# Two-layer encoder: the seam between the first MLP and mixer B with scratch moved, TensorE's order written out and weight splits queued later

## The chip, the core and the metric

The kernel runs on one core of a Trainium2 chip. Its time is the device time of one execution in microseconds; of several executions the median is taken. The profile is of one execution.

## The reference

The input is x (1, 512, 1024) in float32. Two layers follow each other; each is a token mixer and a squared-ReLU MLP, both with a norm ahead and added to the residual. Layer 0 has mixer A (dilated sliding-window attention), layer 1 has mixer B (latent attention), which is where the change lies:

```python
def mla_mixer(h, w_in, q_a_gain, w_qb, kv_a_gain, w_kvb, q_gain, k_gain, w_o):
    lat = h @ w_in                                   # (512, 448)
    c_q, c_kv, k_rope = lat[..., :256], lat[..., 256:384], lat[..., 384:]
    q = (rms_norm(c_q, q_a_gain) @ w_qb).reshape(B, S, 8, 192)
    kv = (rms_norm(c_kv, kv_a_gain) @ w_kvb).reshape(B, S, 8, 256)
    k_nope, v = kv[..., :128], kv[..., 128:]
    k = concatenate([k_nope, broadcast(k_rope)], -1)
    q, k = rms_norm(q, q_gain), rms_norm(k, k_gain)
    ... # rope on the last 64 of q and k
    ... # softmax(q k / sqrt(192)) v over all 512 positions, then @ w_o

def reference(x, ...):
    for i in range(2):
        x = x + mixer_i(rms_norm(x, norm_mix[i]), ...)
        x = x + sq_relu_mlp(rms_norm(x, norm_ffn[i]), ffn_w1[i], ffn_w2[i])
    return x
```

## The kernel before

Matrices are multiplied in three passes: each operand is split into a high part, which ScalarE copies, and a low part, which VectorE subtracts, and TensorE adds up high times high, high times low and low times high. `load_unit` (lines 151 to 160) loads a piece of a weight matrix into a `raw` buffer (three of them) and splits it into a `whi` and a `wlo` buffer (four each). The 512 positions are four row tiles of 128.

The seam is the stretch from the end of MLP 0 to the first attention scores of mixer B. These steps follow each other in it:

- The last two Winograd products of MLP 0 add their results to `resid`. When a row tile is complete, `done0` calls `norm_tile`, which makes the normed row `xn` (in one of the two `S` buffers of pool `mlp0`) and returns `turn`: eight transposes on TensorE in two halves, and the split of their result into `hT`. `done0` calls the turn at once.
- `run_block` on line 1166 multiplies `hT` by `b_w_in`: per row tile four steps of six matmuls, 448 columns wide, 24 matmuls in all, into one of the four `acc` accumulators. `evac_lat` then takes a row: three squares with sums on ScalarE, a root by a power on GpSimd (`rstd_of`, line 133), the normed latents `cn` on VectorE with the gains `gl`, three transposes, and the split into `cT`.
- `new_pair(p)` loads and splits the two weight pieces of heads 2p and 2p+1. `kv_chunk` projects one row of keys and values (three matmuls of 512 columns), takes two squares, the power, `ks`, `kd`; its second part transposes them (four transposes) and splits them into `kn` and `kr`. `q_chunk` does the same for one row of queries (six matmuls of 384 columns).
- The loop over `s_` runs 32 scores (five matmuls each) with maximum, exponential, scaling, four transposes three steps later, and the product with the values after each fourth. While a pair's scores run, the chunks of the next pair are made.

Each engine has one queue, filled in an order that a planner works out when the kernel is built: of what it takes to be ready, the first traced goes first. `tc.issue_after(ins)` ties what is traced in its block, on the engine of `ins`, behind `ins` in that queue; a tie is an order and no wait for a result. In `block_groups` the dictionary `between` gives a function that is traced behind the step with that number, tied behind the step's last matmul; if it returns an instruction, the next step is tied behind it.

Memory: pools are a stack. `h1p` holds `hT_f0`, the normed input of MLP 0 (32 KiB per partition), and `mlp0` lies above it with `a2` (16 KiB), four `asp` (32 KiB) and two `S` (8 KiB). When both are closed, `bpool` (17.5 KiB) and `bw` (71.5 KiB) take their place from the bottom, so `bw` as a whole reaches from the last part of `hT_f0` over `a2`, `asp` and `S`. `gl` uses the one buffer of tag `gain`, which until then holds the gains of the mixer's norm.

Of the kernel before, what the change touches and what calls it, by code (L numbers as in the profile page):

```python
# [10 lines left out]
F32 = mybir.dt.float32  # L11
# [77 lines left out]
def encoder_kernel(ctx: ExitStack, tc: tile.TileContext, x, norm_mix, norm_ffn, a_w_qkv, a_q_gain, a_k_gain,  # L89
# [7 lines left out]
    def nm(s):  # L97
        uid[0] += 1
        return f"{s}_{uid[0]}"
# [24 lines left out]
    def transpose(o, i):  # L124
        return PE.transpose(o, i, ident)  # L125
# [832 lines left out]
    with tc.tile_pool(name="mlp0", bufs=1, reuse_waits="tile") as mp:  # L958
        state = {}

        def done0(r, c):
            state[r] = state.get(r, 0) + 1
            if state[r] < 2:
                return
            if r == 0:
                state["g"] = gain_table(norm_mix[1:2, :].rearrange("o d -> (o d)"), D, "g_mix1")
                state["hT"] = new_hT()
            norm_tile(r, resid[:, r], state["g"], state["hT"], mp, xn_tag="S")()
        mlp(0, ffn_w1[0], ffn_w2[0], hT, resid, mp, done0)
# [4 lines left out]
    if True:  # L974
        with tc.tile_pool(name="bpool", bufs=1, reuse_waits="tile") as bp, \
                tc.tile_pool(name="bw", bufs=2, reuse_waits="tile") as bw:
            cosB = ck[:, C_COSB:C_SINB].rearrange("p (r d) -> p r d", r=NT)
            sinB = ck[:, C_SINB:C_COSA].rearrange("p (r d) -> p r d", r=NT)
            gl = gp.tile([P, D], F32, tag="gain", name="gl")
# [20 lines left out]
            def evac_lat(r, acc):  # L1000
                junk = bw.tile([P, QL], F32, tag="junkb", name=nm("junkb"), bufs=1)
                ss = st.tile([P, 8], F32, tag="lss", name=nm("lss"))
                mean_square(junk, acc[:, 0:QL], QL, ss[:, 0:1])
                mean_square(junk[:, 0:KVL], acc[:, QL:QL + KVL], KVL, ss[:, 1:2])
                mean_square(junk[:, 0:RD], acc[:, 384:448], QKD, ssr[:, r:r + 1])
                V.tensor_scalar(ssr[:, r:r + 1], ssr[:, r:r + 1], EPS, None, op0=ALU.add)
                rs = rstd_of(ss[:, 0:2], 2, EPS, "lrs")
                cn = bw.tile([P, QL + KVL], F32, tag="cn", name=nm("cn"))
                V.scalar_tensor_tensor(cn[:, 0:QL], acc[:, 0:QL], rs[:, 0:1], gl[:, 0:QL], op0=ALU.mult, op1=ALU.mult)
                V.scalar_tensor_tensor(cn[:, QL:384], acc[:, QL:384], rs[:, 1:2], gl[:, QL:384], op0=ALU.mult,  # L1010
                                       op1=ALU.mult)
                t2 = bw.tile([P, 2 * RD], F32, tag="kr2", name=nm("kr2"), bufs=1)[:, 0:RD]
                V.tensor_tensor(krr[:, r], acc[:, 384:448], cgB[:, r, 1], op=ALU.mult)
                V.tensor_tensor(t2[:, 0:32], acc[:, 416:448], sgB[:, r, 1, 32:64], op=ALU.mult)
                V.tensor_tensor(t2[:, 32:64], acc[:, 384:416], sgB[:, r, 1, 0:32], op=ALU.mult)
                G.tensor_tensor(krr[:, r], krr[:, r], t2, op=ALU.add)
                tp = tp_p.tile([P, 512], F32, tag="tp", name=nm("tp"))
                for j in range(3):
                    transpose(tp[:, j * P:(j + 1) * P], cn[:, j * P:(j + 1) * P])
                tv = tp[:, :384].rearrange("p (k t) -> p k t", k=3)  # L1020
                hi, lo = cT[:, :, 0, r * P:(r + 1) * P], cT[:, :, 1, r * P:(r + 1) * P]
                A.activation(hi, tv, AF.Copy)
                V.tensor_tensor(lo, tv, hi.bitcast(F32), op=ALU.subtract)
# [6 lines left out]
            def new_pair(p):  # L1030
# [7 lines left out]
                d["wkv"] = load_unit(wkv[:, :, 512 * p:512 * p + 512], 1, None, 512, home=homes[1])  # L1038
                d["wq"] = load_unit(wq[:, :, 384 * p:384 * p + 384], 2, None, 384, home=homes[0])
# [19 lines left out]
            def q_chunk(d, r):  # L1059
# [3 lines left out]
                junk = bw.tile([P, QL], F32, tag="junkb", name=nm("junkb"), bufs=1)  # L1063
# [5 lines left out]
                qs = bw.tile([P, 2, DH], F32, tag="qs", name=nm("qs"), bufs=2)  # L1069
# [29 lines left out]
            def kv_chunk(d, r):  # L1099
                acc = proj(d, "wkv", r, 2, 512)  # L1100
                a4 = acc.rearrange("p (h c d) -> p h c d", h=2, c=2)
                junk = bw.tile([P, QL], F32, tag="junkb", name=nm("junkb"), bufs=1)
# [5 lines left out]
                ks = bw.tile([P, 2, DH], F32, tag="ks", name=nm("ks"), bufs=2)  # L1108
# [20 lines left out]
            def score(d, h, r):  # L1129
# [11 lines left out]
                pe = bw.tile([P, S], F32, tag="pe", name=nm("pe"), bufs=3)  # L1141
                A.activation(pe, sc, AF.Exp, bias=mx[:, 1:2], scale=rq, accum_out=mx[:, 2:3])
# [23 lines left out]
            run_block(w_units(b_w_in[0], 0, 448), [4], 448, act_stationary(hT, 448), evac_lat)  # L1166
            oB = new_hT()
            cur = new_pair(0)
            late = []
            for r in range(NT):  # L1170
                late.append(kv_chunk(cur, r))
                if r == 2:
                    late.append(q_chunk(cur, 0))
                if r:
                    late.pop(0)()
# [74 lines left out]
```

## Time and profile before

| | us |
|---|---|
| median of 3 runs | 1406.21 |
| lowest and highest | 1405.14 and 1407.54 |
| profiled execution, its own time | 1405.79 |
| its span, first to last instruction | 1404.0 |

Times in the views are counted from the first instruction. TensorE (PE), VectorE (DVE), ScalarE (ACT), GpSimd (POOL) and SyncE (SP) work at the same time; an engine's idle time matters only where the chain that ends last runs through it. The time of a matmul in a view holds its way through the array, so that neighbours overlap; what one costs in a row of many is read from the chain.

### The profile page before, as it was taken

To read this page: it belongs to the slowest core of one execution; us is meant where nothing else is said; L and a number is where in the kernel's file an instruction comes from. 1 tells how busy PE (TensorE), PEld (TensorE's weight loads), DVE (VectorE), ACT (ScalarE), POOL (GpSimd) and SP (SyncE) were. 2 spreads that over 40 slices of the span, in tenths; PEclk is the share of its full clock that TensorE was granted. 3 is DMA by queue.
4 is the path that set the end of the run, shared out by engine and by line. 5 is a ranking of instruction groups with operands and counts; after the bars stand their busy time and mean duration, and the time that the engine had idled before them with its cause. 6 is when DMAs were issued, how large, how long until landed. Compare 5 with 4: busy or idle time off the path is not lost.

```text
span 1404.0 us, 18978 instructions
## 1 busy us (share of the span) xinstructions
PE 1371.9 (98%) x6852; PEld 1164.1 (83%) x6852; DVE 940.9 (67%) x1498; ACT 801.2 (57%) x1643; POOL 225.3 (16%) x240
## 2 busy tenths in 40 slices
PE   7999999999999999999999999999999999999998
PEld 6999878888889989888888878777769888888886
DVE  6885777788788744574655769788745465574747
ACT  6543778687786625454536455777534553644543
POOL 1110212121122001020200204433201020020101
PEclk9999999999999999999999999999999999999999
DMA  9535554655555539486583944201116668493835
GB/s 301 172 133 162 131 135 98 164 124 133 143 125 123 159 106 260 142 187 176 121 238 86 235 96 94 61 31 31 46 46 191 170 132 228 100 226 124 200 85 120
DMA packets 171775, 197.83 MB, mean 141 GB/s; under 512 B 59105, under 2 KB 109025, under 8 KB 171681
## 3 DMA queue, kind: packets, MB, share of 16 engines
q1 hardware_dynamic: 152496, 157.55, 37.9%
q0 software_dynamic: 19184, 39.07, 15.5%
q8 instruction: 54, 0.88, 0.3%
q14 instruction: 41, 0.33, 0.1%
HBM read 176.13 MB, written 7.86 MB: 131 GB/s over the span
## 4 chain that ended last, share of the span: by engine, by line
PE 81%; DVE 7%; ACT 4%; DMA 4%; issue 2%; SPq 0%; POOL 0%; ACTq 0%; DVEq 0%
PE acc L188 46%; PE sc L868 11%; PE tp L868 7%; PE tp L125 3%; DMA xT<-t 2%; PE sc L430 2%; PE acc L1161 1%; PE sc L1055 1%; DVE wlo L811 1%; PE acc L1137 1%; PE tp L430 1%; PE sco L710 1%; PE acc L430 1%; PE sco L706 1%; ACT junk L138 1%
## 5 line engine op out<-in xcount | busy, mean ns | idle before, releaser
L188 PE MATMUL acc<-whi,hT 128*128 128x512 f32 (+2 forms) x1208 | 377.2, 388 | 1.9 <-ACT hT L752 1.0
L188 PE MATMUL acc<-hT_f,whi 128*128 128x512 f32 (+1 forms) x1152 | 317.4, 366 | 0.0
L159 DVE TENSOR_TENSOR wlo<-raw,whi 128x1024 fp32r<-128x1024 f32 (+3 forms) x146 | 172.9, 1188 | 164.3 <-ACT whi L158 163.7
L188 PEld LDWEIGHTS acc<-whi,hT 128*128 128x128 f32 x1208 | 224.3, 188 | 43.0 <-ACT hT L1163 1.5
L158 ACT ACTIVATE whi<-raw 128x1024 fp32r<-128x1024 f32 (+3 forms) x146 | 149.6, 1029 | 161.8 <-PE acc L188 72.1
L188 PEld LDWEIGHTS acc<-hT_f,whi 128*128 128x128 f32 x1152 | 207.8, 189 | 34.9
L188 PE MATMUL acc<-wlo,hT 128*128 128x512 f32 (+2 forms) x604 | 233.0, 387 | 0.7 <-DVE wlo L159 0.7
L811 DVE TENSOR_TENSOR wlo<-wqs,whi 128x1024 fp32r<-128x1024 f32 x112 | 137.7, 1231 | 112.9 <-ACT whi L810 112.9
L810 ACT ACTIVATE whi<-wqs 128x1024 fp32r<-128x1024 f32 x112 | 118.3, 1059 | 161.6 <-PE acc L188 65.0
L188 PE MATMUL acc<-hT_f,wlo 128*128 128x512 f32 (+1 forms) x576 | 204.1, 366 | 0.0
L868 PE MATMUL sc<-whi,asp 128*128 128x512 f32 x512 | 165.2, 390 | 1.3 <-DVE resid L842 1.3
L796 POOL DMA_DIRECT2D wqs<-in_ffn_w_dram x64 | 77.6, 1347 | 540.1 <-DVE wlo L811 358.3
L188 PEld LDWEIGHTS acc<-wlo,hT 128*128 128x128 f32 x604 | 113.6, 188 | 20.2 <-DVE wlo L159 1.1
L188 PEld LDWEIGHTS acc<-hT_f,wlo 128*128 128x128 f32 x576 | 108.3, 189 | 17.4
L868 PEld LDWEIGHTS sc<-whi,asp 128*128 128x128 f32 x512 | 96.2, 188 | 21.9 <-issue 2.1
L868 PE MATMUL tp<-whi,asp 128*128 128x512 f32 x352 | 112.2, 390 | 0.9 <-DVE resid L842 0.9
L133 POOL TENSOR_TENSOR qrs<-rs_v,nhalf 128x4 f32<-128x4 f32 x48 | 65.9, 1376 | 264.1 <-DVE rs_v L130 233.2
L868 PE MATMUL sc<-wlo,asp 128*128 128x512 f32 x256 | 99.7, 390 | 0.0
L304 ACT ACTIVATE qkT<-xT 128x1024 uint16<-128x1024 uint16 x48 | 56.4, 1182 | 42.1 <-DMA xT<-t 42.0
L868 PEld LDWEIGHTS tp<-whi,asp 128*128 128x128 f32 x352 | 66.1, 188 | 15.0 <-DVE resid L842 1.3
L868 PE MATMUL tp<-wlo,asp 128*128 128x512 f32 x176 | 68.2, 390 | 0.0
L138 ACT ACTIVATE junk<-acc 128x128 f32<-128x128 f32 x192 | 52.1, 272 | 10.7 <-PE acc L188 7.0
(236 smaller groups left out, 2187.2 us busy)
## 6 DMA issues: line engine op xcount, KB each, us to landing
wqs<-in_ffn_w_dram SPq DMA_DIRECT2D x80, 512.0 KB, 5.2
raw<-in_ffn_w_dram SPq DMA_DIRECT2D x64, 512.0 KB, 4.2
wqs<-in_ffn_w_dram POOLq DMA_DIRECT2D x64, 512.0 KB, 7.5
raw<-in_a_w_qkv_dram SPq DMA_DIRECT2D x96, 256.0 KB, 3.2
b<-in_a_w_qkv_dram SPq DMA_DIRECT2D x24, 384.0 KB, 5.7
vall<-vo POOLq DMA_DIRECT2D x24, 192.0 KB, 2.3
raw<-in_a_w_o_dram SPq DMA_DIRECT2D x8, 512.0 KB, 3.8
raw<-in_b_w_o_dram SPq DMA_DIRECT2D x8, 512.0 KB, 3.8
```

What stands on the lines that cost most here:

```text
L125: return PE.transpose(o, i, ident)
L133: G.tensor_tensor(out, v[:, :n], nhalf[:, :n], op=ALU.pow)
L138: A.activation(junk, x, AF.Square, scale=1.0 / math.sqrt(dim), accum_out=out)
L158: A.activation(hi[:, :nk, :n], raw[:, :nk, :n], AF.Copy)
L159: V.tensor_tensor(lo[:, :nk, :n], raw[:, :nk, :n], hi[:, :nk, :n].bitcast(F32), op=ALU.subtract)
L188: last = PE.matmul(accs[o][:, oc], lhsT=lt, rhs=rt, start=(kt == 0 and p_i == 0 and hv == 0), stop=(kt == total - 1 and p_i == 2), skip_gr ...
L304: A.activation(dst, xT.rearrange("p (h c) t -> p c t h", h=2), AF.Copy)
L430: PE.matmul(banks[t][:, :VH], lhsT=lt, rhs=rt[:, j], start=(first and k == 0 and i_ == 0), stop=(k == 3 and i_ == 2), skip_group_check=True)
L796: marks["sum"] = nc.gpsimd.dma_start(t, src, accum_op=ALU.add).ins
L810: A.activation(hi, x, AF.Copy)
L811: V.tensor_tensor(lo, x, hi.bitcast(F32), op=ALU.subtract)
L868: PE.matmul(bk[t], lhsT=lt, rhs=rt[:, j], start=(first and k == 0 and i_ == 0), stop=(k == 3 and i_ == 2), skip_group_check=True)
```

## The change

Four things are changed. A new pool `bl` is opened between `bpool` and `bw`; it holds `gl`, the scratch of the latents (`junkb`, `kr2`), `qs`, `ks`, and one tag `pe` of three buffers that the latents' `cn` share with the exponentials. It takes 13.5 KiB, so it ends 1 KiB below the end of what `hT_f0` was, and `bw` begins behind it. `done0` keeps the turns of rows 2 and 3 instead of calling them. `evac_lat` ends ahead of its transposes and returns them as a function; the block of the latents gets a `between` that names when each turn, each latent row's transposes and the first keys are issued by TensorE. And `new_pair` loads both of its pieces first and, for every pair but the first, ties ScalarE's half of the splits behind the first exponential of the pair that is running.

```diff
-            norm_tile(r, resid[:, r], state["g"], state["hT"], mp, xn_tag="S")()
+            turn = norm_tile(r, resid[:, r], state["g"], state["hT"], mp, xn_tag="S")
+            if r < 2:
+                turn()
+            else:
+                state[f"turn{r}"] = turn
...
+                tc.tile_pool(name="bl", bufs=2, reuse_waits="tile") as bl, \
...
-            gl = gp.tile([P, D], F32, tag="gain", name="gl")
+            gl = bl.tile([P, 512], F32, name="gl", bufs=1)
...
-                cn = bw.tile([P, QL + KVL], F32, tag="cn", name=nm("cn"))
+                cn = bl.tile([P, S], F32, tag="pe", name=nm("cn"), bufs=3)
...
-                tp = tp_p.tile([P, 512], F32, tag="tp", name=nm("tp"))
-                for j in range(3):
-                    transpose(tp[:, j * P:(j + 1) * P], cn[:, j * P:(j + 1) * P])
...
+                def turn():
+                    tp = tp_p.tile([P, 512], F32, tag="tp", name=nm("tp"))
+                    for j in range(3):
+                        t = transpose(tp[:, j * P:(j + 1) * P], cn[:, j * P:(j + 1) * P])
...
+                    return t.ins
+                return turn
...
-                d["wkv"] = load_unit(wkv[:, :, 512 * p:512 * p + 512], 1, None, 512, home=homes[1])
-                d["wq"] = load_unit(wq[:, :, 384 * p:384 * p + 384], 2, None, 384, home=homes[0])
+                srcs = ("wkv", wkv[:, :, 512 * p:512 * p + 512], 1, 512), ("wq", wq[:, :, 384 * p:384 * p + 384], 2, 384)
+                raws = [load_raw(src, nk, None, n) for _, src, nk, n in srcs]
+                with ExitStack() as behind:
+                    if p:
+                        behind.enter_context(tc.issue_after(marks["exp", 0, 0]))
+                    for i, (name, src, nk, n) in enumerate(srcs):
+                        d[name] = load_unit(src, nk, None, n, home=homes[1 - i], raw=raws[i])
...
-                A.activation(pe, sc, AF.Exp, bias=mx[:, 1:2], scale=rq, accum_out=mx[:, 2:3])
+                marks["exp", h, r] = A.activation(pe, sc, AF.Exp, bias=mx[:, 1:2], scale=rq, accum_out=mx[:, 2:3]).ins
...
-            run_block(w_units(b_w_in[0], 0, 448), [4], 448, act_stationary(hT, 448), evac_lat)
+            lat, late = {}, []
+
+            def first_pair():
+                t = state["turn2"]()
+                state["cur"] = new_pair(0)
+                return t
+
+            def keys(r):
+                late.append(kv_chunk(state["cur"], r))
+
+            run_block(w_units(b_w_in[0], 0, 448), [4], 448, act_stationary(hT, 448),
+                      lambda r, acc: lat.update({r: evac_lat(r, acc)}),
+                      between={4: first_pair, 7: lambda: lat[0](), 8: state["turn3"], 10: lambda: keys(0),
+                               11: lambda: lat[1](), 13: lambda: late.pop(0)(), 14: lambda: keys(1),
+                               15: lambda: lat[2]()})
             oB = new_hT()
-            cur = new_pair(0)
-            late = []
-            for r in range(NT):
-                late.append(kv_chunk(cur, r))
-                if r == 2:
-                    late.append(q_chunk(cur, 0))
-                if r:
-                    late.pop(0)()
+            cur = state["cur"]
+            late.append(q_chunk(cur, 0))
+            keys(2)
+            late.pop(0)()
+            lat[3]()
+            keys(3)
             for f in late:
                 f()
```

`junkb`, `kr2`, `qs`, `ks` and `pe` go from `bw` to `bl` in the same way. The steps of the block count 0 to 15: step 4r + u is unit u of row r.

## Rows read from the trace of the kernel before

**Rows 1.** The page: busy time of each engine, and the chain that ended last, by engine

```profile
PE 1371.9 (98%) x6852; PEld 1164.1 (83%) x6852; DVE 940.9 (67%) x1498; ACT 801.2 (57%) x1643; POOL 225.3 (16%) x240
...
PE 81%; DVE 7%; ACT 4%; DMA 4%; issue 2%; SPq 0%; POOL 0%; ACTq 0%; DVEq 0%
```

**Rows 2.** Windows around the seam: from:to, length, busy of each engine, clock, DMA

```profile
870.00:882.00 12.00, 12.00 (x68) 11.00 (x68) 6.32 (x10) 4.28 (x10) 0.55 (x1) 1.00 0.41 124
...
888.00:904.00 16.00, 13.10 (x73) 10.44 (x72) 13.69 (x48) 13.84 (x60) 10.90 (x18) 1.00 0.40 128
...
904.00:920.00 16.00, 14.60 (x78) 11.32 (x77) 14.16 (x45) 12.30 (x46) 6.43 (x11) 1.00 0.02 7
...
920.00:950.00 30.00, 30.00 (x154) 22.88 (x154) 26.13 (x76) 22.50 (x74) 8.98 (x14) 1.00 0.11 33
...
950.00:1000.00 50.00, 46.91 (x235) 35.01 (x234) 42.92 (x121) 36.88 (x124) 17.29 (x25) 1.00 0.11 32
```

**Rows 3.** TensorE in order of time, 838 to 930: start, length, what, [idle before]

```profile
871.69 0.37 PE L188 MATMUL acc<-whi,hT 128*128 128x448 f32 x1
...
887.90 0.45 PE L188 MATMUL acc<-whi,hT 128*128 128x448 f32 x1
...
894.46 0.33 PE L125 MATMUL tp<-ck,ks 128*128 128x128 f32 x1 [0.59 <-DVE ks L1109]
...
900.04 1.29 PE L1055 MATMUL sc<-w,cT 128*128 128x384 f32 x6 [0.89 <-DVE r L1076]
...
902.92 0.47 PE L1055 MATMUL sc<-whi,cT 128*128 128x512 f32 x1 [0.65 <-DVE rs_v L130]
...
903.69 0.86 PE L1137 MATMUL acc<-kn,qn 128*128 128x512 f32 x3
```

**Rows 4.** ScalarE in order of time, 850 to 925

```profile
880.96 0.60 ACT L234 ACTIVATE hT<-tp 128x512 fp32r<-128x512 f32 x1 [2.08 <-PE tp L125]
...
881.45 0.38 ACT L138 ACTIVATE junkb<-acc 128x256 f32<-128x256 f32 x1
...
889.84 0.85 ACT L158 ACTIVATE whi<-raw 128x768 fp32r<-128x768 f32 x1 [0.42 <-DVE cT L1023]
...
908.69 0.77 ACT L1142 ACTIVATE pe<-acc,bmx,rqs 128x512 f32<-128x512 f32 x1
```

**Rows 5.** The DMA issues of SyncE's queue in order of time, 830 to 925

```profile
874.73 0.55 SPq L980 DMA_DIRECT2D gl<-in_b_q_a_gain_dram  x1
```

**Rows 6.** The chain in order of time, 860 to 881: start, length, instructions

```profile
863.12 2.74 PE sc L868 x12
...
872.06 0.44 PE tp L125 x4
```

**Rows 7.** VectorE in order of time, 850 to 925

```profile
883.68 0.48 DVE L1009 SCALAR_TENSOR_TENSOR cn<-acc,lrs,gl 128x256 f32<-128x256 f32 x1
...
884.08 0.34 DVE L1010 SCALAR_TENSOR_TENSOR cn<-acc,lrs,gl 128x128 f32<-128x128 f32 x1
...
885.83 2.36 DVE L159 TENSOR_TENSOR wlo<-raw,whi 128x512 fp32r<-128x512 f32 x3
...
890.72 0.96 DVE L159 TENSOR_TENSOR wlo<-raw,whi 128x768 fp32r<-128x768 f32 x1 [0.47 <-ACT whi L158]
```

**Rows 8.** Tile cT: what wrote it; min, median, max ns; first and last start

```profile
L1022 ACT ACTIVATE cT<-tp x4: 482/488/493, 888.2 to 894.3; 128x384 fp32r<-128x384 f32 x4
...
L1023 DVE TENSOR_TENSOR cT<-tp,cT x4: 545/546/556, 889.2 to 894.8; 128x384 fp32r<-128x384 f32 x4
```

**Rows 9.** Groups by line and shape, 880 to 932: busy us, mean ns, idle before

```profile
L1111 POOL TENSOR_TENSOR kd<-krr,krs 128x256 f32<-128x256 f32 x8 | 4.9, 615 | 0.4
...
L1122 ACT ACTIVATE kn<-tp,gn 128x256 fp32r<-128x256 f32 x8 | 3.9, 489 | 0.0
```

**Rows 10.** Line L133, the power on GpSimd: min, median, max ns

```profile
L133 POOL TENSOR_TENSOR nrs<-rs_v,nhalf x16: 548/552/1644, 6.0 to 1073.4; 128x1 f32<-128x1 f32 x16
...
L133 POOL TENSOR_TENSOR krs<-rs_v,nhalf x16: 695/698/862, 892.7 to 986.5; 128x2 f32<-128x2 f32 x16
```

More of the change, by code (lines that the diff above doesn't have):

```diff
@@ L1000, in evac_lat @@
             def evac_lat(r, acc):
-                junk = bw.tile([P, QL], F32, tag="junkb", name=nm("junkb"), bufs=1)
+                junk = bl.tile([P, QL], F32, tag="junkb", name=nm("junkb"), bufs=1)
                 ss = st.tile([P, 8], F32, tag="lss", name=nm("lss"))
@@ L1011, in evac_lat @@
                                        op1=ALU.mult)
-                t2 = bw.tile([P, 2 * RD], F32, tag="kr2", name=nm("kr2"), bufs=1)[:, 0:RD]
+                t2 = bl.tile([P, 2 * RD], F32, tag="kr2", name=nm("kr2"), bufs=1)[:, 0:RD]
                 V.tensor_tensor(krr[:, r], acc[:, 384:448], cgB[:, r, 1], op=ALU.mult)
@@ L1016, in evac_lat @@
                 G.tensor_tensor(krr[:, r], krr[:, r], t2, op=ALU.add)
-                tp = tp_p.tile([P, 512], F32, tag="tp", name=nm("tp"))
-                for j in range(3):
-                    transpose(tp[:, j * P:(j + 1) * P], cn[:, j * P:(j + 1) * P])
[L1020 to L1023, printed above, removed]
+                def turn():
+                    tp = tp_p.tile([P, 512], F32, tag="tp", name=nm("tp"))
+                    for j in range(3):
+                        t = transpose(tp[:, j * P:(j + 1) * P], cn[:, j * P:(j + 1) * P])
+                    tv = tp[:, :384].rearrange("p (k t) -> p k t", k=3)
+                    hi, lo = cT[:, :, 0, r * P:(r + 1) * P], cT[:, :, 1, r * P:(r + 1) * P]
+                    A.activation(hi, tv, AF.Copy)
+                    V.tensor_tensor(lo, tv, hi.bitcast(F32), op=ALU.subtract)
+                    return t.ins
+                return turn
             wq = b_w_qb[0].rearrange("(k p) c -> p k c", p=P)
@@ L1062, in q_chunk @@
                 a3 = acc[:, :384].rearrange("p (h d) -> p h d", h=2)
-                junk = bw.tile([P, QL], F32, tag="junkb", name=nm("junkb"), bufs=1)
+                junk = bl.tile([P, QL], F32, tag="junkb", name=nm("junkb"), bufs=1)
                 ss = st.tile([P, 8], F32, tag="qss", name=nm("qss"))
@@ L1068, in q_chunk @@
                 rstd_of(ss[:, 0:2], 2, QKD * EPS, None, d["rq"][:, r])
-                qs = bw.tile([P, 2, DH], F32, tag="qs", name=nm("qs"), bufs=2)
+                qs = bl.tile([P, 2, DH], F32, tag="qs", name=nm("qs"), bufs=2)
                 A.activation(qs, a3[:, :, 0:DH], AF.Copy)
@@ L1101, in kv_chunk @@
                 a4 = acc.rearrange("p (h c d) -> p h c d", h=2, c=2)
-                junk = bw.tile([P, QL], F32, tag="junkb", name=nm("junkb"), bufs=1)
+                junk = bl.tile([P, QL], F32, tag="junkb", name=nm("junkb"), bufs=1)
                 ss = st.tile([P, 8], F32, tag="kss", name=nm("kss"))
@@ L1107, in kv_chunk @@
                 A.activation(d["v"][:, r], a4[:, :, 1], AF.Copy)
-                ks = bw.tile([P, 2, DH], F32, tag="ks", name=nm("ks"), bufs=2)
+                ks = bl.tile([P, 2, DH], F32, tag="ks", name=nm("ks"), bufs=2)
                 V.tensor_tensor(ks, a4[:, :, 0], rs.unsqueeze(2).broadcast_to([P, 2, DH]), op=ALU.mult)
@@ L1140, in score @@
                 V.tensor_scalar(mx[:, 1:2], mx[:, 0:1], rq, -1.0, op0=ALU.mult, op1=ALU.mult)
-                pe = bw.tile([P, S], F32, tag="pe", name=nm("pe"), bufs=3)
-                A.activation(pe, sc, AF.Exp, bias=mx[:, 1:2], scale=rq, accum_out=mx[:, 2:3])
+                pe = bl.tile([P, S], F32, tag="pe", name=nm("pe"), bufs=3)
+                marks["exp", h, r] = A.activation(pe, sc, AF.Exp, bias=mx[:, 1:2], scale=rq, accum_out=mx[:, 2:3]).ins
                 V.reciprocal(mx[:, 3:4], mx[:, 2:3])
```

## The prediction

> **What bounds the kernel now.** The page comes first: TensorE is busy for 98% of the span, and 81% of the chain that ends last is TensorE's own work [rows 1]. A change that leaves TensorE's instructions as they are, as this one does, can only win time in which TensorE stands. The second view is therefore the table of windows: where does TensorE stand, and what do the others do there? From 870 to 882 it is busy for all of 12.00 us, while VectorE works 6.32 and ScalarE 4.28. From 888 to 904 it works 13.10 of 16, and now VectorE (13.69) and ScalarE (13.84) are the full ones; from 904 to 920 it works 14.60 of 16 [rows 2]. So the seam loses 2.9 + 1.4 = 4.3 us, and just ahead of the loss two engines are half idle. The clock is 1.00 in all these windows; it plays no part.
>
> The third view is the order of time. The last matmul of latent row 0 starts at 871.69, so row 0 is complete at 871.9 [rows 3]. Its first square starts on ScalarE only at 881.45, right behind the copy of the last normed row's transposes, for which ScalarE had stood 2.08 us [rows 4]. Row 0 waits 9.6 us in an accumulator while the engines that could take it stand. Then the evacuations of four rows come at once, and TensorE stands at 894.46, 900.04 and 902.92 until VectorE is through [rows 3]. The first score starts at 903.69.
>
> What held row 0 is not a transfer: its squares read the accumulator and write `junkb`. I read it from the memory plan: `bw` reaches over the `S` buffers, and the last `xn` in them is read until the transposes just before 880.96. The normed latents had a second hold, `gl`, loaded only from 874.73 on because its buffer still held the mixer's gains [rows 5].
>
> **The change part by part.**
>
> *The pool `bl`.* It lies within what `hT_f0` held, which was last read before the seam, so the squares and `cn` need not wait for `xn`; `gl`'s two small loads leave the place behind the weight loads in SyncE's queue and go out early. Neither adds an instruction.
>
> *TensorE's order.* 12 matmuls of 512 columns take 2.74 us, 0.23 each, and four transposes 0.44, 0.11 each [rows 6]. By width a matmul of 448 columns takes 0.20 and a step of six 1.2. Everything in TensorE's queue behind a tied transpose waits with it, so each tie needs slack.
> - Row 0: from its first square to the end of `cn` it took 884.08 + 0.34 - 881.45 = 3.0 us [rows 4, 7]. From 871.9 that gives 874.9. TensorE reaches `lat[0]` after step 4 (1.2), eight transposes (0.9) and steps 5 to 7 (3.6), at 877.6. Slack 2.7.
> - Rows 1 and 2 have four steps and more between end and transposes: slack above 2.5.
> - Keys of row 0: two squares, sum and power take 883.68 - 881.45 = 2.2 as for the latents, then `kd` 0.6 [rows 9], together 2.8 or 2.9; between projection and transposes lie three steps and three transposes, 3.9. Slack 1.0, the smallest.
>
> I take no stall; if ScalarE's or VectorE's queue adds over 1.0 us to the last, TensorE stands for the excess.
>
> *The first score.* Row 3 ended at 888.1. Ahead of it now lie row 1's transposes (0.33), two key projections (6 x 0.23 = 1.4) and the first keys' transposes (0.44): it ends 2.1 later, at 890.2. From there: squares to `cn` 3.0; transposes 0.33, copy 0.49, difference 0.55 [rows 8], with handing over 1.6; keys of row 3 0.7 and 0.2; squares, power and `kd` 2.9; transposes 0.44, `kn` copied in 0.49 [rows 9] and subtracted in as much, with handing over 1.6. Sum 10.0: the score can't start before 900.2. The same way took 15.6 before (888.1 to 903.7), of which 5.6 was queueing on engines 86% busy [rows 2]. Three rows' evacuation and the splits (ScalarE 0.85, VectorE 0.96 and 2.36 here [rows 4, 7]) have left this stretch, so I take about a third of the queueing, 1.8: first score at 902.0, **1.7 earlier**. Bounds: 3.5 without queueing, 0 with all of it.
>
> *Work done by then.* From 890.2 to 902.0 TensorE has 11.8 us for 9.2 us of work that needs no score: all four query rows with their transposes among it. Against before, three rows' transposes (12 x 0.11 = 1.3) are banked and pair 1's first keys (3 x 0.23 = 0.7; at 902.92 before) are not: **0.6**. Bounds -0.7 and 1.3.
>
> *Splits held back.* Pair 1's splits now stand behind the exponential that came at 908.69, 5.0 after its score [rows 3, 4], then ScalarE needs up to 0.85 for each and VectorE 0.8 and 1.0. No pair 1 work is there to fill TensorE until about 1.5 after the exponential. It has four scores of 1.1 to go on with, 4.5 us. If the exponential stays at 5.0, TensorE stands 2.0 or more; if VectorE, freed of the query rows, gives the maximum at once, nothing. Before, it stood 1.4 there. I take 1.0: **0.4 won**, bounds -1.0 and 1.4. Pair 2's splits move from 888 into pair 1's scores, where VectorE works 26.13 of 30 and TensorE stands nowhere although a split lies there already [rows 2]; nearest to that row I take 0. The bound on the other side is the whole of two pairs' splits, ScalarE 0.85 and by width 0.6, VectorE 0.96 and 0.8 (2.36 for three), 3.2 each, 6.4 us.
>
> *The sum.* 1.7 + 0.6 + 0.4 = 2.7. The profiled execution took 1405.79 with a span of 1404.0; it would take 1403.1. The median of the runs is 0.42 above it: 1406.21 - 2.7 = **1403.5**. About 0.2%, 2.8 us, is what a measurement of this kernel can tell from no change, so the forecast lies on that line.
>
> **GpSimd beside the splits.** Line 133's power takes 0.552 in the median for one element and once 1.644; with two elements 0.698 and up to 0.862 [rows 10]. Something on VectorE can hold it. [...] By rows alone: each of four splits (0.8 and 1.0 twice) holds one power that is on the path, 3.6 us, and the sum would be 0.9 slower, 1407.1. I give it little, since those powers serve the next pair and have several us to spare.
>
> **The rivals.**
> 1. *As summed*, 1403.5; its own range 1401.9 to 1405.2. For it: 9.6 us of a finished row unattended beside idle engines. Chance 0.58, of which 0.33 passes 2.8 us.
> 2. *All of the seam comes back*: TensorE stands nowhere from 888 to 920, 4.3 us, 1401.9, and if the 3.1 us lost from 950 to 1000 [rows 2] shrink as well, down to 1400. Against it: row 3's chain of 10.0 us has only 9.2 of work beside it. Chance 0.12.
> 3. *The wait moves*: the first score is earlier, but TensorE then stands for pair 1's keys, the 2.0 above or more. 1.7 + 0.6 - 1.6 = 0.7, 1405.5. Chance 0.13.
> 4. *GpSimd is shut out*, 1407.1. Chance 0.03.
> 5. *Slower*: the held splits decide. In pairs 0 and 1 VectorE already works 14.16 of 16 [rows 2]; a split ahead of a maximum delays its exponential, the accumulator it frees, and the next score. In full that costs 6.4 against 2.7 won: 1409.9. It decides from 5.5 us on, and below that the result is no change. For it: TensorE does stand from 950 to 1000, where VectorE works 42.92 of 50 [rows 2]. Against it: 920 to 950. Chance 0.14.
>
> **Chances and range.** Faster by over 0.2%: 0.33 + 0.12 = 0.45. Within: 0.25 + 0.13 + 0.03 = 0.41. Slower: 0.14. The range runs from 1400.8, which leaves out a small part of case 2 (0.05), to 1408.4, which leaves out most of case 5 (0.13).
>
> **What would show it.** Right: the first `junkb` of the latents starts near 872 to 874, not 9.6 us after its row; ScalarE and VectorE are busier from 870 to 882 and less from 888 to 904; the transposes of `cn` follow steps 7, 11 and 15 without idle time ahead; the first score starts from 901 to 903. Wrong: idle time ahead of a tied transpose; the first square still behind the last normed row, which would refute my reading of the memory; idle time after the fourth score until a `whi` of pair 1; powers of over 0.9 us next to a split; or a seam that is shorter while 920 to 1000 becomes longer by as much.

## The result and the profile after

The changed kernel takes 1409.34 us (median of ten runs, 1408.16 to 1409.98) against 1405.47 for the kernel before, measured beside it. The ratio is 1.0026, 95% interval 1.0017 to 1.0035: slower by 3.7 us, where 2.7 us less was forecast, and above the top of the range. One of the ten runs of the kernel before took 3571.98 us; the ratio leaves it out. In the tables below a ratio's last digit, 0.0001, is 0.14 us.

The page first: each engine's busy time, then the chain that ended last, by engine.

```profile
PE 1374.7 (98%) x6852; PEld 1164.7 (83%) x6852; DVE 938.0 (67%) x1498; ACT 801.5 (57%) x1643; POOL 227.4 (16%) x240
...
PE 74%; DVE 7%; DMA 7%; ACT 6%; issue 5%; SPq 0%; POOL 0%; ACTq 0%; DVEq 0%; POOLq 0%
```

TensorE issues the same 6852 matmuls, and its busy time is 2.8 us longer [rows 1]. A matmul's record is longer when the clock is lower (2.27 us against 1.29 for six of them, below), so that is already a hint. Windows around the seam (from:to, length, busy time of TensorE, its weight loads, VectorE, ScalarE and GpSimd, then the granted clock, the DMA share and GB/s), with four windows of 2 us behind them:

```profile
870.00:882.00 12.00, 12.00 (x70) 11.13 (x69) 9.18 (x25) 6.37 (x20) 2.60 (x5) 1.00 0.49 151
...
888.00:904.00 16.00, 11.77 (x64) 9.76 (x64) 9.01 (x34) 10.70 (x47) 8.35 (x14) 0.96 0.00 1
904.00:920.00 16.00, 15.39 (x73) 11.70 (x72) 13.60 (x41) 11.56 (x40) 6.72 (x10) 0.93 0.14 41
920.00:950.00 30.00, 28.05 (x139) 20.93 (x140) 25.05 (x75) 21.59 (x74) 10.37 (x15) 1.00 0.10 31
950.00:1000.00 50.00, 47.91 (x247) 35.94 (x246) 42.83 (x126) 39.08 (x127) 16.80 (x24) 1.00 0.16 53
...
900.00:902.00 2.00, 0.00 (x0) 0.00 (x0) 1.61 (x5) 2.00 (x12) 1.17 (x2) 1.00 0.00 0
902.00:904.00 2.00, 1.66 (x8) 1.69 (x9) 1.32 (x8) 1.47 (x6) 1.80 (x4) 0.69 0.04 8
904.00:906.00 2.00, 2.00 (x9) 1.80 (x8) 0.93 (x5) 0.81 (x3) 1.14 (x2) 0.50 0.00 0
906.00:908.00 2.00, 2.00 (x13) 1.65 (x11) 1.23 (x4) 1.41 (x5) 0.59 (x1) 0.95 0.00 0
```

Against [rows 2]: from 870 to 882 VectorE works 9.18 instead of 6.32 and ScalarE 6.37 instead of 4.28, and from 888 to 904 both have lost a quarter to a third of their load. That is what was forecast. But TensorE works less there too, 11.77 instead of 13.10, and it loses another 2.0 us from 920 to 950, where it was full. And the clock column, 1.00 everywhere before, falls to 0.50. By the three windows that show it, taken as 0.50 or 1.00 throughout, the half clock lasts 0.31/0.50 x 2 + 2 + 0.05/0.50 x 2 = 3.4 us.

TensorE in order of time (start, length, line, output and inputs, shape, count, idle time before and what ended it):

```profile
891.38 0.37 PE L188 MATMUL acc<-whi,hT 128*128 128x448 f32 x1
...
895.47 1.29 PE L1069 MATMUL sc<-w,cT 128*128 128x384 f32 x6 [0.82 <-ACT kn L1136]
...
899.24 0.27 PE L125 MATMUL tp<-ck,kd 128*128 128x128 f32 x1
902.34 0.30 PE L125 MATMUL tp<-ck,ks 128*128 128x128 f32 x1 [2.83 <-ACT junkb L1080]
...
902.89 2.27 PE L1069 MATMUL sc<-w,cT 128*128 128x384 f32 x6
904.96 0.63 PE L1151 MATMUL acc<-kn,qn 128*128 128x512 f32 x1
...
910.64 0.74 PE L1069 MATMUL sc<-whi,cT 128*128 128x512 f32 x2
```

Row 3's last latent matmul starts at 891.38, not at 887.90 [rows 3]. Ahead of the last keys' transposes TensorE stands 2.83 us, the longest stand of the seam in either kernel. Right behind it six matmuls of a query row take 2.27, where six of the same shape took 1.29 at 895.47: that is the half clock. The first score starts at 904.96 (before: 903.69), and pair 1's first keys at 910.64, behind the third of the five matmuls of the third score (before: 902.92, ahead of the first). ScalarE, and SyncE's DMA queue:

```profile
872.52 0.37 ACT L138 ACTIVATE junkb<-acc 128x256 f32<-128x256 f32 x1
...
909.19 0.78 ACT L1156 ACTIVATE pe<-acc,bmx,rqs 128x512 f32<-128x512 f32 x1 [0.58 <-DVE bmx L1154]
...
909.96 1.35 ACT L158 ACTIVATE whi<-raw 128x512 fp32r<-128x512 f32 x2
```

```profile
824.95 0.34 SPq L985 DMA_DIRECT2D gl<-in_b_q_a_gain_dram  x1
```

The latents' first square starts at 872.52 instead of 881.45 [rows 4], and their gain is loaded 50 us earlier [rows 5]: the memory's part works. Pair 1's two splits (one row, two instructions: the view groups them under the first shape) stand right behind the first exponential.

### The profile page after: what moved, and what is told of

Same layout as the page of the kernel before. It is cut to its first block, busy times and chain, and to the rows that moved or that the text cites. A ratio compares the mean times of both kernels' runs of the same rounds, so it can differ in the third digit from the quotient of the medians.

```text
span 1407.5 us, 18971 instructions
## 1 busy us (share of the span) xinstructions
PE 1374.7 (98%) x6852; PEld 1164.7 (83%) x6852; DVE 938.0 (67%) x1498; ACT 801.5 (57%) x1643; POOL 227.4 (16%) x240
## 3 DMA queue, kind: packets, MB, share of 16 engines
q1 hardware_dynamic: 152496, 157.55, 37.8%
q0 software_dynamic: 19184, 39.07, 15.6%
## 4 chain that ended last, share of the span: by engine, by line
PE 74%; DVE 7%; DMA 7%; ACT 6%; issue 5%; SPq 0%; POOL 0%; ACTq 0%; DVEq 0%; POOLq 0%
PE acc L188 44%; PE sc L868 9%; PE tp L868 6%; DMA xT<-t 3%; PE tp L125 3%; PE sc L430 2%; DMA wqs<-in_ffn_w_dram 2%; PE acc L1175 2%; DVE wlo L811 1%; PE tp L430 1%; PE sc L1069 1%; ACT junk L138 1%; PE acc L1151 1%; PE acc L430 1%; PE sco L710 1%
## 5 line engine op out<-in xcount | busy, mean ns | idle before, releaser
L133 POOL TENSOR_TENSOR qrs<-rs_v,nhalf 128x4 f32<-128x4 f32 x48 | 66.0, 1376 | 264.8 <-DVE rs_v L130 234.0
```

The costliest lines, as they stand in the source:

```text
L133: G.tensor_tensor(out, v[:, :n], nhalf[:, :n], op=ALU.pow)
```

## The experiments

Each was run in five rounds beside the kernel before; ratios are against that. First undo or isolate one part at a time.

**Hold-back undone.** The hold-back is the tie of a pair's splits behind the first exponential of the pair that is running. The changed kernel without it:

```diff
-                    if p:
-                        behind.enter_context(tc.issue_after(marks["exp", 0, 0]))
```

> The changed kernel with the hold-back alone undone: the splits of pairs 1 to 3 are free again, pool and ties stay. Theory A (TensorE's tied order: row 3's latents are complete late, nothing is queued to cover the wait for the last keys, and the stand of 2.83 us is followed by half clock until 906.3): pair 1's projections still stand behind the last keys' transposes in TensorE's queue, so the stand and the half clock stay; 1408.5 to 1409.5. Theory B (the held splits decide, the prediction's rival 5): all 3.7 us come back, 1405.5 or less, and the stretch from 920 to 1000 is as short as before.

Measured 1409.32 us, ratio 1.0030 (1.0018 to 1.0041): nothing comes back. Its stands with 1.5 us and more, and three of its windows:

```profile
893.95 0.52 PE L125 MATMUL tp<-ck,cn 128*128 128x128 f32 x3 [1.57 <-DVE cn L1014]
...
901.95 0.30 PE L125 MATMUL tp<-ck,ks 128*128 128x128 f32 x1 [2.83 <-ACT junkb L1078]
```

```profile
894.00:896.00 2.00, 1.80 (x9) 1.62 (x10) 1.96 (x8) 0.65 (x2) 1.43 (x3) 0.84 0.20 76
896.00:898.00 2.00, 2.00 (x8) 1.61 (x8) 0.42 (x1) 0.00 (x0) 0.90 (x2) 0.50 0.00 0
...
902.00:904.00 2.00, 2.00 (x9) 2.00 (x10) 1.12 (x8) 1.11 (x4) 2.00 (x3) 0.55 0.04 8
```

With the splits back in the seam there are two stands and two stretches at half clock, 6.8 us together. Theory A as I had written it (order alone) looked right here.

**Hold-back alone**, in the kernel before:

> The kernel before with the hold-back alone: both loads of a pair are issued first, the splits of pairs 1 to 3 wait for the exponential. Theory A: only the cover of pair 1's first keys (0.65 us ahead of the first score) is lost, 1405.5 to 1406.7, granted clock 1.00 throughout. Theory B: slower by about as much as the change, 1408.5 to 1409.5.

Measured 1407.68, ratio 1.0021 (1.0012 to 1.0030), and the granted clock is 1.00 in all windows of the seam: neither theory. The hold-back costs 2.9 us without the pool and without a tie of TensorE's order.

**Pool alone**: the memory moves, every transpose is called at once, the planner's own order, no hold-back.

```diff
             turn = norm_tile(r, resid[:, r], state["g"], state["hT"], mp, xn_tag="S")
-            if r < 2:
-                turn()
-            else:
-                state[f"turn{r}"] = turn
+            turn()
...
-                      lambda r, acc: lat.update({r: evac_lat(r, acc)}),
-                      between={4: first_pair, 7: lambda: lat[0](), 8: state["turn3"], 10: lambda: keys(0),
-                               11: lambda: lat[1](), 13: lambda: late.pop(0)(), 14: lambda: keys(1),
-                               15: lambda: lat[2]()})
+                      lambda r, acc: evac_lat(r, acc)())
...
+            for r in range(NT):
+                late.append(kv_chunk(cur, r))
```

> The changed kernel with the pool alone: latents' scratch in bl, every transpose called at once and the planner's own order on TensorE, no hold-back. Theory A: the latents are evacuated from 872 on and row 3 is complete at 888, not at 891.6; the first score comes at 901.5 to 903 and the time is 1403.5 to 1405.0. Theory C (the pool itself costs, since its buffers hold later weights or scores back): 1407 or more, with a first score no later than in the kernel before.

Measured 1405.12, ratio 1.0001 (0.9992 to 1.0010): no change. Its first latent matmul and first score, its first square of row 0, and the first latent matmul of the kernel before:

```profile
864.68 0.36 PE L188 MATMUL acc<-whi,hT 128*128 128x448 f32 x1
...
902.49 1.16 PE L1146 MATMUL acc<-kn,qn 128*128 128x512 f32 x3
```

```profile
871.08 0.36 ACT L138 ACTIVATE junkb<-acc 128x256 f32<-128x256 f32 x1
```

```profile
865.69 0.36 PE L188 MATMUL acc<-whi,hT 128*128 128x448 f32 x1
```

The first score comes 37.8 us after the first latent matmul, and in the kernel before it is 38.0 [rows 3]. Row 0's first square starts at 871.08, and evacuating the first rows some 9 us earlier moves the first score by 0.2. So the pool costs nothing, against theory C, and wins nothing, against the forecast.

**Ties of the transposes without the keys ahead**, with and without the hold-back:

```diff
-                      between={4: first_pair, 7: lambda: lat[0](), 8: state["turn3"], 10: lambda: keys(0),
-                               11: lambda: lat[1](), 13: lambda: late.pop(0)(), 14: lambda: keys(1),
-                               15: lambda: lat[2]()})
+                      between={4: state["turn2"], 7: lambda: lat[0](), 8: state["turn3"], 11: lambda: lat[1](),
+                               15: lambda: lat[2]()})
...
```

> The changed kernel with only the transposes tied: keys of rows 0 and 1 and query row 0 are issued behind the latents again, as in the kernel before; pool and hold-back stay. Theory A: row 3 is complete at about 889 (two key projections, a key transpose and most of a query row leave its way), the first score comes at about 902.5, no stand above 1.5 us ahead of it and no half clock; 1405.5 to 1407.0. Theory B: the hold-back is still there, 1408.5 or more.

> The tied transposes without the keys ahead and without the hold-back: pool and ties of latents' and norms' transposes alone. After the first four runs I hold two costs to be there (theory D): the hold-back lengthens the way from the first score to the last (128.2 us before; 131.0, 131.2 and 132.5 in the three kernels with it), and the tied order with splits in the seam lengthens the way to the first score (38.0 us from the first latent matmul before, 42.4 without the hold-back). D here: first to last score 128.5, first score at 38.5 to 40, 1405.5 to 1407.5. If the ties of transposes alone cost as much as with the keys, 1409.

With the hold-back 1409.42, ratio 1.0032 (1.0021 to 1.0043); without it 1406.45, ratio 1.0008 (0.9999 to 1.0016). Here the hold-back does cost, 3.4 us. Theory A falls: taking the keys out of row 3's way gives nothing while the hold-back is there. But A had also expected the long stand and the half clock to go with the keys, and the kernel with the hold-back still has both:

```profile
903.67 0.30 PE L125 MATMUL tp<-ck,ks 128*128 128x128 f32 x1 [2.31 <-DVE kr L1140]
```

```profile
904.00:906.00 2.00, 2.00 (x9) 1.62 (x8) 0.84 (x4) 1.25 (x4) 0.00 (x0) 0.50 0.00 0
```

Its half clock lasts 3.4 us again; in the kernel without the hold-back the clock is 1.00 in all windows of the seam. So a part of these 3.4 us can be the clock.

**Which pair's hold.** In the kernel with the pool alone, the hold-back for pair 1 only, as here, or for pairs 2 and 3 only (`if p > 1:`):

```diff
+                    if p == 1:
+                        behind.enter_context(tc.issue_after(marks["exp", 0, 0]))
```

> The pool alone, with the hold-back for pair 1's splits only (pairs 2 and 3 free). D: pair 1's weights come too late to cover pair 0's scores, 1407 to 1408.5. If it is the splits of the later pairs among the scores that cost (the prediction's rival 5), no more than 1405.8.

> The pool alone, with the hold-back for the splits of pairs 2 and 3 only (pair 1 free). D: pair 1's keys cover TensorE as before and two pairs' splits are out of the seam or do no harm, 1404.5 to 1405.8. If the splits of the later pairs among the scores cost, 1407 or more.

Pair 1 held: 1409.52, ratio 1.0025 (1.0014 to 1.0035). Pairs 2 and 3 held: 1403.51, ratio 0.9990 (0.9981 to 0.9999). One condition separates a loss of 3.4 us from a gain of 1.5. In the kernel with pair 1 held, TensorE from pair 1's first keys on, and the window that begins 0.47 us behind its first score:

```profile
907.32 0.73 PE L1066 MATMUL sc<-whi,cT 128*128 128x512 f32 x2
...
916.53 0.50 PE L1066 MATMUL sc<-whi,cT 128*128 128x512 f32 x1 [0.99 <-DVE ks L1120]
...
923.25 0.41 PE L1066 MATMUL sc<-whi,cT 128*128 128x384 f32 x1 [1.35 <-DVE ks L1120]
```

```profile
902.87:918.87 16.00, 14.38 (x70) 10.47 (x70) 15.30 (x43) 12.91 (x41) 4.86 (x7) 1.00 0.33 99
```

Its first score starts at 902.40, as early as in the kernel with the pool alone (902.49), and the clock is 1.00 in all windows of the seam. Then two of the next projections of pair 1 wait, 0.99 and 1.35 us, until VectorE has taken the keys of one ahead out of its bank (`ks`): the projections come closer together than VectorE, busy 15.30 of 16 us there, can follow.

**What in the hold costs.** Two kernels, each with one half of it on top of the pool alone: the splits stay in the seam and only TensorE's first key projection of pair 1 is put where the hold-back put it; or the real splits stay, and two more of the same size stand behind the exponential.

```diff
...
+                        if p == 0 and c == 2:
+                            behind.enter_context(tc.issue_after(marks["sc", 0, 2]))
                         fresh = [fn(nxt, r) for fn, r in plan.get(c, [])]
```

```diff
+                    if s_ == 2:
+                        with tc.issue_after(marks["exp", 0, 0]):
+                            for src, hi, lo in (...):
+                                A.activation(hi, src, AF.Copy)
+                                V.tensor_tensor(lo, src, hi.bitcast(F32), op=ALU.subtract)
```

> The pool alone, no hold-back, every split in the seam as in that kernel; only pair 1's first key projection on TensorE is tied behind the third matmul of pair 0's third score, where the hold-back put it (907.3 in the kernel with pair 1's splits held). If the hold-back costs because pair 1's keys are late on TensorE (nothing covers pair 0's scores, then everything of pair 1 comes close together), 1408 to 1409.5, as with pair 1's splits held. If it costs because the splits take ScalarE's and VectorE's time among pair 0's scores, no change from the pool alone: 1404.5 to 1405.8.

> The pool alone, no hold-back, and two more splits of the sizes of a pair's two loads behind the exponential of pair 0's first score: a copy on ScalarE and a subtraction on VectorE each, into a part of the output tile that is overwritten later; nothing waits for them. They add to the work, and take the engines where the hold-back put pair 1's splits, while pair 1's real weights are ready early. If engine time among the scores is what costs, ScalarE's 1.45 and VectorE's 1.8 us show: 1406.7 to 1408. If late keys are what costs, 1405.0 to 1406.0.

Late keys: 1405.95, ratio 1.0008 (0.9999 to 1.0017), 1.0 us above the pool alone. Splits among the scores: 1406.31, ratio 1.0013 (1.0004 to 1.0022), 1.7 above it. By their medians each takes a part, together 2.7 of the 3.4. But each difference is uncertain by some 1.8 us (two intervals of 0.0009 either way): neither part is clear of zero, both times lie outside what either reading had expected, and the two may as well be all of the 3.4. So the division is not shown. The profiled execution with late keys also has a stretch at half clock (below), so its 1.0 may be partly that.

**The hold for pairs 2 and 3 without the pool**:

> The kernel before with the hold-back for the splits of pairs 2 and 3 only, without the pool. With the pool it measured 1403.5 against 1405.2. If the gain is that of splits moved out of the seam, it is there without the pool too: 1403.3 to 1404.7, perhaps a little more, since the seam is fuller without the pool. If pool and hold-back are needed together, 1405.0 to 1406.0.

Measured 1406.86, ratio 1.0014 (1.0005 to 1.0023): slower, against both expectations. The same hold-back wins 1.5 us with the pool and loses 2.0 without it. I have no shown cause; a changed set of free instructions gives the planner another order for everything behind it, and that holds for every pair of kernels here that differ in a hold.

**The clock.** Needless matmuls in the place of the stand of 2.83 us, first into the bank of the transposes behind it:

```diff
                     tp = tp_p.tile([P, 512], F32, tag="tp", name=nm("tp"))
+                    if d["p"] == 0 and r == 3:
+                        for i in range(10):
+                            PE.matmul(tp, lhsT=cT[:, 2, 0, 384:512], rhs=w0[:, 1, 0, 0, :], start=(i == 0), stop=(i == 9))
```

> The changed kernel with ten more matmuls of 512 columns (2.3 us) on TensorE, ahead of the last keys' transposes and into the same bank, whose result those transposes overwrite: work that the computation does not need, in the place of the stand of 2.83 us. If the half clock of 3.41 us that follows the stand costs time (up to 1.7 us), the granted clock stays at 1.00 here and the time falls to 1407.3 to 1408.5, although more work is done. If TensorE waits for others there anyway, the time stays at 1409 or rises.

Measured 1410.76, ratio 1.0036 (1.0024 to 1.0048). The fill missed, and the kernel is 1.4 us slower than the changed one: the matmuls waited 1.93 us for their bank, and the ten then took 4.12 us. Below, with the granted clock at 1.00, the same ten take 2.54, so I read this as half clock for most of the way:

```profile
901.99 4.12 PE L1132 MATMUL tp<-w,cT 128*128 128x512 f32 x10 [1.93 <-DVE qr L1110]
```

The same ten matmuls into an accumulator that had been free for long (`pre`, which the first score takes next):

```diff
...
+                    with tc.issue_after(marks["turned"]):
+                        state["pre"] = acc_p.tile([P, 512], F32, tag="acc", name="pre")
+                        for i in range(10):
+                            PE.matmul(state["pre"], lhsT=cT[:, 2, 0, 384:512], rhs=w0[:, 1, 0, 0, :], ...)
```

> The changed kernel with ten more matmuls of 512 columns right behind the transposes of the third keys, into a bank that has long been free (the first try waited 1.93 us for its bank and ran at half clock). TensorE's order is otherwise that of the changed kernel; the stand of 2.83 us shrinks to about 0.6. If that stand brings the half clock, it stays 1.00 here and the time falls by up to 1.7 us, 1407.6 to 1409; if the half clock is not what costs, 1409 to 1409.8.

Measured 1406.47, ratio 1.0012 (1.0003 to 1.0021): ten more matmuls, and 2.0 us less. Its rows at the same place, and its window there:

```profile
889.52 0.37 PE L188 MATMUL acc<-whi,hT 128*128 128x448 f32 x1
...
897.42 2.54 PE L1209 MATMUL pre<-w,cT 128*128 128x512 f32 x10
900.50 0.30 PE L125 MATMUL tp<-ck,ks 128*128 128x128 f32 x1 [0.54 <-ACT junkb L1080]
...
901.00 1.30 PE L1069 MATMUL sc<-w,cT 128*128 128x384 f32 x6
902.14 0.40 PE L1152 MATMUL pre<-kn,qn 128*128 128x512 f32 x1
...
907.27 0.73 PE L1069 MATMUL sc<-whi,cT 128*128 128x512 f32 x2
```

```profile
902.00:904.00 2.00, 2.00 (x13) 1.63 (x12) 1.62 (x8) 1.79 (x8) 1.32 (x2) 1.00 0.00 0
```

Row 3's last latent matmul starts at 889.52 in this execution, so the last keys' transposes come 900.50 - 889.52 = 10.98 us behind it, in the changed kernel 902.34 - 891.38 = 10.96. The fill delays nothing, and the query row behind the transposes takes 1.30 instead of 2.27. By pair 1's first keys, 907.27 - 889.52 = 17.75 us behind row 3 instead of 910.64 - 891.38 = 19.26, the filled kernel is 1.5 us ahead: that much of the 2.0 stands in the two traces.

**The rest of the table.** Four kernels that set the causes against each other:

> The changed kernel without the hold-back, whose two stands of 1.57 and 2.83 us were followed by two stretches at half clock (6.82 us together) and a first score at 42.4 us from the first latent matmul: five more matmuls go into the first stand and ten into the second (3.4 us of work that is not needed), TensorE's order otherwise unchanged. If the tied order costs through the clock, both stretches go, up to 3.4 us come back and the time is 1406 to 1407.5. If it costs because ScalarE and VectorE are behind anyway, the stands move and the time stays at 1408.5 to 1410.

> The changed kernel with the hold-back for pairs 2 and 3 only; pair 1's splits are free. In the kernel with the pool alone this one change gave 1.4 us, and holding pair 1's cost 4. If pair 1's hold is half of the loss by itself, 1406 to 1407.5; if the tied order's stand and half clock decide (the stand of 2.8 us ahead of the last keys' transposes is in TensorE's order here too), 1407.8 to 1409.5.

> Pool, ties of the transposes alone (keys behind the latents) and the hold-back for pairs 2 and 3. The pool with that hold-back measured 1403.5, the ties of transposes cost 1.2 without a hold-back. Sum of the two: 1404.7, range 1403.5 to 1406. If the ties lead to a stand and half clock here as in the kernel that held all pairs, 1406.5 or more.

> As the changed kernel with the hold-back for pairs 2 and 3 only, and the ten matmuls into a free bank ahead of the last keys' transposes. If clock and pair 1's hold are the two halves of the loss, both are gone: 1404 to 1405.5, at the kernel before or under it. If the seam still costs through ScalarE and VectorE, 1406 or more.

No hold-back, both stands filled: 1407.17, ratio 1.0017 (1.0008 to 1.0025). Hold-back for pairs 2 and 3 only (`if p > 1:`): 1404.31, ratio 1.0000 (0.9991 to 1.0009). The same with the transposes tied and the keys behind the latents: 1404.87, ratio 1.0001 (0.9993 to 1.0010). And with all ties and the stand filled: 1403.63, ratio 0.9987 (0.9978 to 0.9996). All ratios, by order (down) and hold-back (across):

| | none | pair 1 | pairs 2, 3 | all |
|---|---|---|---|---|
| kernel before | 1 | | 1.0014 | 1.0021 |
| pool | 1.0001 | 1.0025 | 0.9990 | |
| pool, transposes tied | 1.0008 | | 1.0001 | 1.0032 |
| pool, all ties | 1.0030 | | 1.0000 | 1.0026 |
| pool, all ties, stand filled | 1.0017 | | 0.9987 | 1.0012 |

Each difference of two ratios is uncertain by some 0.0013, 1.8 us, so what counts is that several agree. Holding pair 1's splits costs 0.0024, 0.0031, 0.0026 and 0.0025 (pair 1 against none, or all against pairs 2 and 3). The first and the last compare kernels whose profiles show no half clock in the seam: 3.4 and 3.5 us. The 0.0031 has the half clock of the kernel with all pairs held in it, and its partner has none.

Filling TensorE's stand gives 0.0013, 0.0013 and 0.0014 (no hold-back, pairs 2 and 3, all): 1.8 to 2.0 us, although it adds work. For the changed kernel 3.4 us at half clock explain 1.7 of that: all ten of its executions show a granted clock of 0.999 over the span, and all eleven of the filled one 1.000. The other two do not fit so well. Without the hold-back 6.8 us at half clock went, half of which, 3.4, should come back. And with pairs 2 and 3 held, six of the eleven executions without the fill show 1.000, where 3.4 us at half clock would make it 0.9988: they had no such stretch. Those six took 1404.13 us in the mean, the other five 1405.36, and the filled kernel 1403.44. So the clock is a part of what the fill gives there, and what the rest is stays open.

One way from the kernel before to the changed one goes by single steps: pool 0.0001, pairs 2 and 3 held -0.0011, all ties +0.0010, pair 1 held +0.0026, in all 0.0026.

The last step in two profiles: windows of the kernel with pairs 2 and 3 held, set 2.54 us earlier than those of the changed kernel because its first latent matmul is that much earlier, and its TensorE rows.

```profile
885.46:901.46 16.00, 11.76 (x64) 9.75 (x63) 10.28 (x36) 11.55 (x48) 8.68 (x14) 0.95 0.15 42
901.46:917.46 16.00, 16.00 (x87) 13.61 (x87) 13.75 (x42) 11.64 (x44) 7.78 (x12) 0.94 0.00 1
917.46:947.46 30.00, 29.41 (x149) 22.06 (x148) 26.02 (x80) 23.00 (x76) 10.67 (x15) 1.00 0.10 31
```

```profile
899.84 0.36 PE L125 MATMUL tp<-ck,ks 128*128 128x128 f32 x1 [2.83 <-ACT junkb L1080]
...
902.77 0.63 PE L1151 MATMUL acc<-kn,qn 128*128 128x512 f32 x1
...
904.31 0.39 PE L1069 MATMUL sc<-whi,cT 128*128 128x512 f32 x1
```

Up to the first score these two executions are the same: the same stand, 3.5 and 3.4 us at half clock, 11.76 and 11.77 busy of 16. Then pair 1's first keys come 1.5 us behind the first score instead of 5.7. In the next 46 us this kernel's TensorE issues 236 recorded matmuls and stands 0.6; the changed kernel issues 212 and stands 2.6. The visible stands are 2.0 of 3.7. The rest can lie in waits that the busy column hides, which is not shown: a matmul's record is longer than the distance to the next one (0.27 against 0.11 for a transpose), so a wait shorter than the difference shows as busy time.

## Why the prediction was wrong

**Memory and tied transposes: right, and worth nothing.** First square at 872.52 (forecast 872 to 874), more work from 870 to 882, no idle time ahead of the first three tied transposes. But in the kernel with the pool alone that made the first score 0.2 earlier. I had left only a third of 5.6 us of queueing on row 3's chain, because three rows' evacuation and the splits leave the stretch. The pool alone moves the rows and not the splits; VectorE and ScalarE still work 12.66 and 13.38 of 16 there (13.69 and 13.84 before [rows 2]), and nearly all of the queueing stays:

```profile
886.74:902.74 16.00, 13.72 (x71) 10.29 (x69) 12.66 (x41) 13.38 (x58) 10.33 (x17) 1.00 0.32 98
```

**The first score: 902.0 forecast, 904.96 measured.** Two parts. Row 3 was to end 2.1 later and ended 3.5 later: the planner also put a query row's six matmuls, free to run, among the latents (about 1.1 us), and the first latent matmul itself came 0.25 later. And its chain took 13.4 instead of 11.8 (904.96 - 891.6): 3.4 of the 5.6 us of queueing stayed, where 1.8 was taken, and part of it is the stand with its half clock. The bound was summed wrongly, too: with all of the queueing the first score comes at 890.2 + 15.6 = 905.8, 2.1 later than before, and not at "0". A tie sets what comes before what, not what else may come between.

**"The clock is 1.00 in all these windows; it plays no part": failed.** I had read that off the old trace, although the change makes new stands. In the changed kernel it cost 1.5 us by the traces with and without the fill and 2.0, uncertain by 1.8, by their times. It is not all that the ties cost: with pairs 2 and 3 held, the kernel with the transposes alone tied is at 1.0001 (0.9990 without ties) with the clock at 1.00 in all windows of its seam, and without the hold-back all ties cost 0.0016 over the pool even with both stands filled. In the traces without and with the fill the granted clock went with TensorE's standing: behind the stand of 2.83 us it fell to 0.50, and with ten needless matmuls in that place, which left a stand of 0.54, it is 1.00 from 860 to 1000.

**"Splits held back": the step that failed.** It stood in the sum as 0.4 won for pair 1 and 0 for pair 2. Measured: 3.4 to 3.5 lost for pair 1 where the clock does not differ, and 1.0 to 4.2 won for pairs 2 and 3 in the kernels with the pool. I had the two apart, and looked for the danger at the wrong one. Pair 1's wait was costed as a stand ahead of its own keys, 2.0 in rival 3. TensorE has scores to go on with there and hardly stands; the loss that shows comes later: from 904 to 950 it stands 2.6 us in 46, and 0.6 in the kernel where pair 1 is not held. My reading is that what is lost is the cover (pair 1's projections, which TensorE can do while a score of pair 0 waits), and VectorE's and ScalarE's time for the splits among the scores; the two kernels that took these apart do not show either by itself.

**The rivals.** Rival 5's time, 1409.9, is near the result, and its mechanism (splits take time among the scores) may be about half of it: 1.7 us, uncertain by 1.8, by the kernel with two more splits. But it was argued for the splits held into pairs 0 and 1 as a whole, decided from 5.5 us on, and the later pairs' splits turned out to help, so the nearness of its time is luck. Rival 3's mechanism, late keys, has 1.0 by the median, as uncertain; its sum took 1.6 as lost, where its own stand of 2.0 against 1.4 before gives 0.6. Rival 2 fell: from 888 to 920 TensorE stood 4.8 us, before 4.3. Rival 4 fell: the two-element powers of over 0.9 us after the change start at 913.95, 923.37 and 945.5, 1.00 us long at most, and no split (pair 1's last ends at 912.7, pair 2's at 943.4) lies beside them. A power that takes longer beside splits can be seen in mixer A of the kernel before: one of four elements, 1.00 us at the least, took 3.58 from 338.08 on, with splits of 1.22 us on VectorE from 337.85 and from 339.59.

**What stays open**: how the 3.4 us divide between late keys, splits and the planner's other order, what the fill gives besides the clock, whether the later DMA of the held pairs' weights (pair 2's last load was issued at 911.34, not at 886.54) has a share, and why the hold for pairs 2 and 3 loses without the pool.

Two kernels beat both: the pool with only pairs 2 and 3 held (0.9990, its interval just under 1), and the changed kernel with that hold and the stand filled (0.9987).

## What to carry to other kernels

Before work is moved out of a crowded stretch, ask what it was the supply for: a split that is first in line feeds the engine that sets the time, and holding it back cost 3.4 us here; a later one in the same stretch may be held and win, as it did with the pool and did not without it. Tying the order moves free work too and can open one long stand in place of several short ones, so read the granted clock again after any change that makes TensorE stand: here it fell to 0.50 behind a stand of 2.83 us. A few needless matmuls into a free bank are a cheap test of whether a stand's clock is what costs, if the clock of every execution is read beside it: here the fill also gained where most executions had no half clock.

## What the runs showed of the hardware

The granted clock fell to 0.50 behind a single stand of 2.83 us (the changed kernel), but the length of one stand does not tell it. Behind 1.57 us it fell to 0.50 in the kernel without hold-back; behind 1.11 and then 1.58 us it stayed 1.00 in the one with tied transposes and pairs 2 and 3 held:

```profile
898.73 1.28 PE L1069 MATMUL sc<-w,cT 128*128 128x384 f32 x6 [1.11 <-DVE r L1090]
...
902.46 0.47 PE L1069 MATMUL sc<-whi,cT 128*128 128x512 f32 x1 [1.58 <-DVE r L1090]
```

```profile
902.00:904.00 2.00, 1.54 (x10) 1.23 (x11) 1.47 (x6) 1.12 (x5) 0.98 (x2) 1.00 0.00 0
```

In the kernel with late keys it fell to 0.50 although no stand there was over 0.89 us:

```profile
900.00:902.00 2.00, 1.08 (x9) 0.63 (x6) 1.32 (x6) 1.81 (x8) 1.13 (x3) 1.00 0.00 0
902.00:904.00 2.00, 1.34 (x5) 0.81 (x6) 1.94 (x5) 1.01 (x3) 1.38 (x2) 0.93 0.00 0
904.00:906.00 2.00, 2.00 (x9) 1.70 (x8) 0.76 (x4) 0.75 (x2) 0.00 (x0) 0.50 0.03 8
906.00:908.00 2.00, 2.00 (x9) 1.43 (x8) 1.82 (x6) 1.22 (x4) 0.73 (x1) 0.72 0.00 0
```

It can also differ between executions of one kernel: in the one with all ties and pairs 2 and 3 held it fell to 0.50 behind the stand of 2.83 us in the profiled execution, and six of eleven executions show 1.000 over the span, so they had no such stretch. Through such a stretch TensorE is busy for all of its time by the profile (2.00 of 2.00 us from 904 to 906 in the changed kernel), and only the clock column and the length of like instructions (2.27 against 1.29) show that it works more slowly.
